# Fixing the order of TensorE's work in a 64-expert stage with issue dependencies

## The chip, the cores and the metric

The kernel runs on one core of a Trainium2 chip. The time is the device time of the whole program in microseconds, the median of three runs. Beside it stands one profiled execution, from which all rows below come; times in it count from the first instruction.

## The reference, cut to what matters

The program is a block with a mixer and a mixture of experts, followed by two attention layers. The change touches the experts alone. There are 512 tokens of width 1024 and 64 experts; each token goes to two experts, and each expert computes

```
hdn = silu(xblk @ w1[e]) * (xblk @ w3[e])      # 1024 -> 512, twice
y   = hdn @ w2[e]                              # 512 -> 1024
moe = zeros.at[buf_tok].add(yb * buf_w)        # back to the tokens, weighted
```

Every expert's three matrices are float32, 2 MiB each, so the stage reads 384 MiB of weights, whatever the routing.

## The kernel before, in words

`experts()` takes the 64 experts as 32 pairs. A pair holds 64 slots of each of its two experts, 128 rows in all. What a pair does on TensorE (PE):

- **Gather** (`gather`, L994): the pair's token rows are picked by a product of the tokens, split in a high and a low part (`n2h`, `n2l`), with a one-hot matrix `ohr` that `select` (L975 to L982) builds on VectorE. It is done for two pairs at once: 8 column blocks x 2 parts x 4 token blocks = 64 products with 256 columns, into the PSUM tag `pgat` of two buffers, copied out to `xT` by ScalarE (L996).
- **Half-width products** (`pair`): `up` (L1050) multiplies the gathered rows with `w1` and `w3` into `ph`, `down` (L1081) the gated hidden rows with `w2` into `py`. Each product has 64 stationary columns, one half of the array for each expert. A step of `up` or `down` uses one loaded tile `wraw` of 1 MiB and makes four products, which the trace counts as eight matrix instructions. A pair has 8 steps of `up` and 4 of `down`.
- **Turn** (`turn`, L1069): four transposes of the gated hidden rows, between `up` and `down`.
- **Spread** (`spread`, L1003): four transposes of the one-hot matrix per pair give `S`, used to bring results back.
- **Combination** (`combine`, L1108, L1109): for two pairs at once, 8 tiles `pcomb` of four full-width products with 512 columns, each added to `acc` by VectorE (L1111). The tag `pcomb` has two buffers. Its operands `yh` and `yl` are made from `py` by `weigh`: VectorE (L1095), ScalarE (L1096), VectorE (L1097).

The tiles `wraw` are loaded from the queue of SP by `eload` (L1029), one transfer of 1 MiB at a time, into a ring of `RAW = 10` buffers; a transfer waits until the step that used its buffer ten loads earlier is done.

The text of the program gives one order, with a small clock of its own: `later(d, f)` runs `f` after `d` more steps. In it, the work of two pairs is: six `up` steps of an odd pair, the combination of the two pairs that ended before and the gather for the next two, two `up` steps, the spread, four `down` steps of the pair before, eight `up` steps of the next pair, four `down` steps. The order that runs is not that of the text: the tile scheduler places each engine's instructions by its own model of time and by data dependencies. `tc.issue_after(ins)` adds a dependency of order alone, with no semaphore: what is traced inside the block stands behind `ins` on the same engine.

Of the kernel before, what the change touches and what calls it, by code (L numbers as in the profile page):

```python
# [10 lines left out]
F32 = mybir.dt.float32  # L11
# [7 lines left out]
P = 128  # L19
T = 512  # L20
NT = T // P
D = 1024
KD = D // P
# [23 lines left out]
class Kernel:  # L47
    def __init__(self, tc, I, out):
        self.tc, self.nc, self.I, self.out = tc, tc.nc, I, out
        self.rawn = 2048  # L50


    def f(self, name="f", dt=F32, shape=None):
# [914 lines left out]
    def select(self, first, n, sg):  # L968
# [10 lines left out]
        def task(j):  # L979
            u = self.op.tile([P, n * P], F32, tag="oh", name="oh", bufs=4)  # L980
            nc.vector.tensor_scalar(u, io, sg[:, 1, j:j + 1], None, op0=ALU.is_equal)  # L981
            nc.vector.scalar_tensor_tensor(r[:, j].rearrange("t n s -> t (n s)"), io, sg[:, 0, j:j + 1], u, op0=ALU.is_equal, op1=ALU.add)  # L982
        return r, [lambda j=j: task(j) for j in range(NT)]

    def gather(self, oh, n, xT):

        nc = self.nc
        per = 4 // n
        for k0 in range(0, KD, per):
            ps = self.pg.tile([P, per, n, P], F32, tag="pgat", name="pgat")  # L990
            for k in range(per):
                for half, src in enumerate((self.n2h, self.n2l)):
                    for j in range(NT):
                        nc.tensor.matmul(ps[:, k], src[j][:, k0 + k], oh[:, j].rearrange("t n s -> t (n s)"),  # L994
                                         start=half + j == 0, stop=half == 1 and j == NT - 1)
            nc.scalar.copy(xT[:, k0:k0 + per], ps)  # L996

    def spread(self, oh, i, later, loop):

        nc = self.nc  # L1000
        pS = self.pc.tile([P, T], F32, tag="pcomb", name="pcomb")
        for j in range(NT):
            nc.tensor.transpose(pS[:, j * P:(j + 1) * P], oh.bitcast(F32)[:, j, i], self.ident)  # L1003
        S = self.op.tile([P, T], R32, tag="S", name="S", bufs=4 if loop is None else 1)
        later(1, lambda: nc.scalar.activation(S, pS, AF.Copy))
        return S
# [25 lines left out]
    def pair(self, x, ws, later, done, loaded=()):  # L1032


        nc = self.nc
        mm = nc.tensor.matmul
        st, loaded = {}, list(loaded)
        own = [slice(64 * e, 64 * e + 64) for e in range(2)]

        def raws(w, c):  # L1040
            return loaded.pop(0) if loaded else self.eload(ws[w], w, c)

        def up(w, c):
            raw = raws(w, c)
            if c == 0:
                st[w] = self.ph.tile([P, 512], F32, tag=f"ph{w}", name="ph")
            for i in range(2):
                k = 2 * c + i
                for e in range(2):
                    mm(st[w][own[e]], x(k)[:, own[e]], raw[:, e, i], start=k == 0, stop=k == KD - 1, skip_group_check=True)  # L1050
            if c == 3:
                if w == 0:
                    later(1, act)
                else:
                    later(1, gate)
                    later(2, turn)
                    later(3, turned)

        def act():
            st["t"] = self.ep.tile([P, 512], F32, tag="silu", name="silu")  # L1060
            nc.scalar.activation(st["t"], st[0], AF.Silu)

        def gate():
            nc.vector.tensor_tensor(st["t"], st["t"], st[1], op=ALU.mult)  # L1064

        def turn():
            st["pt"] = self.pg.tile([P, 4, P], F32, tag="pgat", name="pht")
            for k in range(4):
                nc.tensor.transpose(st["pt"][:, k], st["t"][:, k * P:(k + 1) * P], self.ident)  # L1069

        def turned():
            st["hT"] = self.ep.tile([P, 4, P], F32, tag="hT", name="hT")
            nc.scalar.copy(st["hT"], st["pt"])

        def down(c):
            raw = raws(2, c)
            if c == 0:
                st["y"] = [self.py.tile([P, 512], F32, tag="py", name="py") for _ in range(2)]
            for q in range(2):
                for e in range(2):  # L1080
                    mm(st["y"][q][own[e]], st["hT"][:, c, own[e]], raw[:, e, 0, q * 512:(q + 1) * 512],  # L1081
                       start=c == 0, stop=c == 3, skip_group_check=True)
            if c == 3:
                later(1, lambda: done(st["y"]))
        return [lambda w=w, c=c: up(w, c) for w in range(2) for c in range(4)], [lambda c=c: down(c) for c in range(4)]

    def weigh(self, py, wcol, later):
# [12 lines left out]
    def combine(self, pairs):  # L1100

        nc = self.nc
        for j in range(NT):
            for q in range(2):
                ps = self.pc.tile([P, T], F32, tag="pcomb", name="pcomb")
                o = slice(q * 512, (q + 1) * 512)
                for i, (S, yh, yl) in enumerate(pairs):
                    nc.tensor.matmul(ps, S[:, j * P:(j + 1) * P], yh[:, o], start=i == 0, stop=False)  # L1108
                    nc.tensor.matmul(ps, S[:, j * P:(j + 1) * P], yl[:, o], start=False, stop=i == len(pairs) - 1)  # L1109
                a = self.acc[:, j, o]  # L1110
                nc.vector.tensor_tensor(a, a, ps, op=ALU.add)  # L1111

# [8 lines left out]
    def experts(self):  # L1121
        nc, I = self.nc, self.I
# [23 lines left out]
        sel, S = {}, {}  # L1146
# [33 lines left out]
        with self.tc.For_i(0, trips, 1):  # L1180
# [12 lines left out]
            for q in range(2):  # L1193
                b, e, ei = lt([P, 1], f"lb{q}"), lt([P, 1], f"le{q}"), lt([P, 1], f"lei{q}", I32)
# [6 lines left out]
            t = lt([P, NT, 64], "lt")  # L1201
# [16 lines left out]
            for k in range(2):  # L1218
                for j in range(NT):
# [3 lines left out]
                                     stop=k == 1 and j == NT - 1)  # L1223
# [9 lines left out]
            flush()  # L1233
            V.tensor_scalar(cur, cur, 1.0, None, op0=ALU.add)
        yield
        self.nload = nload

        prev = []
        for pr in range(32):
# [790 lines left out]
```

## Time and profile before

| | |
|---|---|
| median of three runs | 3038.85 us (3027.07 to 3040.16) |
| profiled execution | 3034.57 us, its span 3032.9 us |
| span before the expert stage | 0 to 862 us |
| expert stage | 862 to 1905 us |
| attention layers | 1905 to 3032.9 us |

The stage's borders are read from the loads of weights (the first that the stage itself issues, at 862 us) and the last product of a combination (1901 us). Share of busy time counts an engine's instructions; a pause of PE between two of its instructions shows only where no instruction runs. In the rows, PE is the matrix products, PEld the loads of their stationary operand, SPq the queue of SP's transfers, and PEclk the granted TensorE clock as a share of the full one.

### The profile page before, as it was taken

To read this page: it belongs to the slowest core of one execution; us is meant where nothing else is said; L and a number is where in the kernel's file an instruction comes from. 1 tells how busy PE (TensorE), PEld (TensorE's weight loads), DVE (VectorE), ACT (ScalarE), POOL (GpSimd) and SP (SyncE) were. 2 spreads that over 40 slices of the span, in tenths; PEclk is the share of its full clock that TensorE was granted. 3 is DMA by queue.
4 is the path that set the end of the run, shared out by engine and by line. 5 is a ranking of instruction groups with operands and counts; after the bars stand their busy time and mean duration, and the time that the engine had idled before them with its cause. 6 is when DMAs were issued, how large, how long until landed. Compare 5 with 4: busy or idle time off the path is not lost.

```text
span 3032.9 us, 37454 instructions
## 1 busy us (share of the span) xinstructions
PE 2847.4 (94%) x14006; PEld 1954.3 (64%) x14006; DVE 1579.9 (52%) x2830; ACT 1099.6 (36%) x2216; POOL 588.1 (19%) x698
## 2 busy tenths in 40 slices
PE   6989999899879999999999999799999999999999
PEld 5877878778644444444444443677888777788877
DVE  5799999646432222222222222666666456657653
ACT  4556555445311111111111111455555335546541
POOL 2257665511210000000000000623100114310001
PEclk9999999999989999999999999898999999989999
DMA  7435444374469999999999998341222344212224
GB/s 231 115 114 165 139 125 129 98 238 137 154 244 400 391 390 394 387 386 385 393 389 397 388 384 313 111 126 29 67 87 78 116 152 128 56 42 84 84 87 149
DMA packets 356786, 627.93 MB, mean 207 GB/s; under 512 B 24000, under 2 KB 205032, under 8 KB 356600
## 3 DMA queue, kind: packets, MB, share of 16 engines
q1 hardware_dynamic: 339680, 601.27, 56.4%
q10 hardware_dynamic: 14360, 15.83, 1.6%
q0 software_dynamic: 2560, 8.39, 0.8%
q8 instruction: 112, 1.84, 0.3%
q14 instruction: 74, 0.61, 0.1%
HBM read 593.95 MB, written 31.47 MB: 206 GB/s over the span
## 4 chain that ended last, share of the span: by engine, by line
PE 64%; DVE 3%; ACT 2%; DMA 1%; issue 1%; POOL 0%; SPq 0%; DVEq 0%; ACTq 0%
PE ph L1050 14%; PE py L1081 8%; PE mm L93 6%; PE mm L94 6%; PE mm L95 6%; PE pgat L994 4%; PE pcomb L1108 2%; PE pcomb L1109 2%; PE o L1549 2%; PE at L95 2%; PE at L93 2%; PE at L94 2%; PE at L1586 1%; PE at L1719 1%; PE at L1568 1%; DVE yl L1097 1%
## 5 line engine op out<-in xcount | busy, mean ns | idle before, releaser
L1050 PE MATMUL ph<-wraw,xT 128*64 128x512 f32 x2048 | 473.0, 601 | 5.6 <-DVE oh L981 5.6
L69 DVE TENSOR_TENSOR wlo<-wraw,whi 128x512 fp32r<-128x512 f32 x466 | 367.4, 796 | 202.4 <-ACT whi L68 189.0
L68 ACT ACTIVATE whi<-wraw 128x512 fp32r<-128x512 f32 x466 | 287.1, 627 | 342.3 <-PE mm L94 262.0
L1050 PEld LDWEIGHTS ph<-wraw,xT 128*64 128x64 f32 x2048 | 137.1, 137 | 270.9 <-issue 267.2
L1081 PE MATMUL py<-wraw,hT 128*64 128x512 f32 x1024 | 240.4, 601 | 0.0
L93 PE MATMUL mm<-hh,whi 128*128 128x512 f32 (+1 forms) x560 | 229.9, 411 | 1.1 <-ACT ga L1649 1.1
L94 PE MATMUL mm<-hl,whi 128*128 128x512 f32 (+1 forms) x560 | 227.4, 406 | 0.0
L95 PE MATMUL mm<-hh,wlo 128*128 128x512 f32 (+1 forms) x560 | 226.3, 404 | 0.0
L93 PE MATMUL mm<-n1h,whi 128*128 128x512 f32 x448 | 183.7, 410 | 24.3 <-DVE c L387 12.1
L1095 DVE SCALAR_TENSOR_TENSOR ys<-py,wslot,g 128x512 f32<-128x512 f32 x64 | 48.0, 751 | 286.0 <-PE py L1081 282.5
L1111 DVE TENSOR_TENSOR acc<-acc,pcomb 128x512 f32<-128x512 f32 x128 | 86.6, 687 | 208.2 <-PE pcomb L1109 208.2
L1292 POOL MEMSET invt<- 128x1 f32 x32 | 1.0, 99 | 942.0 <-DMA wraw<-in_w_dram 942.0
L95 PE MATMUL mm<-n1h,wlo 128*128 128x512 f32 x448 | 180.5, 403 | 0.0
L94 PE MATMUL mm<-n1l,whi 128*128 128x512 f32 x448 | 180.2, 403 | 0.0
L547 DVE SCALAR_TENSOR_TENSOR ucvp<-upad,dwh,ucvp 128x512 f32<-128x512 f32 x232 | 173.4, 747 | 3.7 <-ACT ucvp L541 2.2
L1064 DVE TENSOR_TENSOR silu<-silu,ph 128x512 f32<-128x512 f32 x32 | 22.0, 688 | 258.9 <-PE ph L1050 258.9
L1081 PEld LDWEIGHTS py<-wraw,hT 128*64 128x64 f32 x1024 | 65.7, 136 | 109.6 <-issue 101.4
L93 PEld LDWEIGHTS mm<-hh,whi 128*128 128x128 f32 (+1 forms) x560 | 106.5, 190 | 25.9 <-ACT ga L1649 2.5
L95 PEld LDWEIGHTS mm<-hh,wlo 128*128 128x128 f32 (+1 forms) x560 | 106.3, 190 | 25.5
L94 PEld LDWEIGHTS mm<-hl,whi 128*128 128x128 f32 (+1 forms) x560 | 106.5, 190 | 22.7
L93 PEld LDWEIGHTS mm<-n1h,whi 128*128 128x128 f32 x448 | 87.4, 195 | 45.3 <-DVE c L387 13.6
L93 PE MATMUL mm<-yh,whi 128*128 128x512 f32 x256 | 101.0, 409 | 16.1 <-ACT gb L1649 7.0
(648 smaller groups left out, 6294.2 us busy)
## 6 DMA issues: line engine op xcount, KB each, us to landing
wraw<-in_w_dram SPq DMA_DIRECT2D x384, 1024.0 KB
wraw<-in_w_in_dram SPq DMA_DIRECT2D x164, 512.0 KB
wada<-in_w_ada_dram SPq DMA_DIRECT2D x96, 256.0 KB
wraw<-in_w_ssm_out_dram SPq DMA_DIRECT2D x32, 256.0 KB
wraw<-in_cmp_w_dram SPq DMA_DIRECT2D x16, 512.0 KB
wraw<-in_w_out_dram SPq DMA_DIRECT2D x16, 512.0 KB
zd<-z ACTq DMA_DIRECT2D x32, 128.0 KB
z<-zd SPq DMA_DIRECT2D x16, 256.0 KB
```

What stands on the lines that cost most here:

```text
L68: self.nc.scalar.activation(hi, v, AF.Copy)
L69: self.nc.vector.tensor_sub(lo, v, hi.bitcast(F32))
L93: mm(ps, lh, rh, start=start, stop=False)
L94: mm(ps, lh, rl, start=False, stop=False)
L95: mm(ps, ll, rh, start=False, stop=stop)
L547: nc.vector.scalar_tensor_tensor(st[-1], u[:, k:k + T], self.dwh[:, 8 * k + m:8 * k + m + 1], st[0], op0=ALU.mult, op1=ALU.add)
L994: nc.tensor.matmul(ps[:, k], src[j][:, k0 + k], oh[:, j].rearrange("t n s -> t (n s)"), start=half + j == 0, stop=half == 1 and j == NT - 1)
L1050: mm(st[w][own[e]], x(k)[:, own[e]], raw[:, e, i], start=k == 0, stop=k == KD - 1, skip_group_check=True)
L1081: mm(st["y"][q][own[e]], st["hT"][:, c, own[e]], raw[:, e, 0, q * 512:(q + 1) * 512], start=c == 0, stop=c == 3, skip_group_check=True)
L1108: nc.tensor.matmul(ps, S[:, j * P:(j + 1) * P], yh[:, o], start=i == 0, stop=False)
L1109: nc.tensor.matmul(ps, S[:, j * P:(j + 1) * P], yl[:, o], start=False, stop=i == len(pairs) - 1)
L1111: nc.vector.tensor_tensor(a, a, ps, op=ALU.add)
```

## The change

All full-width work of the expert stage (gather, spread, combination) is put behind the last half-width product traced so far, and every half-width product behind the last full-width one traced so far. So the two kinds follow each other on PE as they do in the text. The products themselves, their number, shapes and operands stay. The transposes of `turn` get no such dependency. `self.half` and `self.whole` are emptied ahead of the loop over the pairs.

```
+    def behind_all(self, last):
+        return self.tc.issue_after(last.ins) if last and self.nload is not None else nullcontext()
...
     def gather(self, oh, n, xT):
...
-                        nc.tensor.matmul(ps[:, k], src[j][:, k0 + k], oh[:, j]...)
+                        with self.behind_all(self.half):
+                            self.whole = nc.tensor.matmul(ps[:, k], src[j][:, k0 + k], oh[:, j]...)
...
     def spread(self, oh, i, later, loop):
...
-            nc.tensor.transpose(pS[:, j * P:(j + 1) * P], oh.bitcast(F32)[:, j, i], self.ident)
+            with self.behind_all(self.half):
+                self.whole = nc.tensor.transpose(pS[:, j * P:(j + 1) * P], oh.bitcast(F32)[:, j, i], self.ident)
...
     up and down in pair():
-                    mm(st[w][own[e]], x(k)[:, own[e]], raw[:, e, i], ...)
+                with self.behind_all(self.whole):
+                    self.half = mm(st[w][own[e]], x(k)[:, own[e]], raw[:, e, i], ...)
...
     def combine(self, pairs):
...
+                with self.behind_all(self.half):
+                    for i, (S, yh, yl) in enumerate(pairs):
+                        nc.tensor.matmul(ps, S[:, j * P:(j + 1) * P], yh[:, o], ...)
+                        self.whole = nc.tensor.matmul(ps, S[:, j * P:(j + 1) * P], yl[:, o], ...)
...
     in experts(), ahead of the loop over the pairs:
-        self.nload = nload
+        self.nload, self.whole, self.half = nload, None, None
```

## Rows read from the trace of the kernel before

**Rows 1.** The page's span in 40 equal slices; busy tenths, then GB/s.

```profile
PE   6989999899879999999999999799999999999999
DMA  7435444374469999999999998341222344212224
GB/s 231 115 114 165 139 125 129 98 238 137 154 244 400 391 390 394 387 386 385 393 389 397 388 384 313 111 126 29 67 87 78 116 152 128 56 42 84 84 87 149
```

**Rows 2.** Waits of PE's weight loads, 865 to 1902 us: total, times, longest.

```profile
PEld pht L1069 <- DVE silu L1064: 27.9, 16, 1.7
PEld ph L1050 <- DMA wraw<-in_w_dram: 1.1, 3, 0.4
```

**Rows 3.** Waits of SP's transfer queue, 865 to 1880 us: total, times, longest.

```profile
SPq L1029 <- PE ph L1050: 520.7, 252, 6.2
```

**Rows 4.** Busy time of each engine in stretches of the expert stage.

```profile
core 0: us, PE busy (x) PEld busy (x) DVE busy (x) ACT busy (x) POOL busy (x), PEclk, DMA share, GB/s
874.00:1875.00 1001.00, 974.75 (x4704) 423.11 (x4702) 230.35 (x398) 119.80 (x185) 0.98 (x32) 1.00 1.01 392
874.00:962.00 88.00, 87.14 (x452) 41.09 (x450) 15.50 (x31) 12.12 (x20) 0.00 (x0) 1.00 1.03 409
1193.90:1258.60 64.70, 63.03 (x306) 27.42 (x306) 15.18 (x25) 7.81 (x12) 0.00 (x0) 1.00 1.01 388
1287.00:1306.00 19.00, 18.93 (x87) 6.92 (x85) 7.18 (x15) 2.56 (x4) 0.00 (x0) 1.00 0.97 345
1888.00:1898.00 10.00, 7.13 (x17) 4.87 (x18) 6.12 (x21) 2.39 (x5) 2.07 (x5) 0.66 0.00 1
```

**Rows 5.** PE in order of time, 1272 to 1326 us: start, length, work.

```profile
1277.61 1.94 PE L1050 MATMUL ph<-wraw,xT 128*64 128x512 f32 x8
...
1280.61 1.94 PE L1050 MATMUL ph<-wraw,xT 128*64 128x512 f32 x8
...
1282.81 0.39 PE L1109 MATMUL pcomb<-yl,S 128*128 128x512 f32 x1
...
1284.20 0.39 PE L1109 MATMUL pcomb<-yl,S 128*128 128x512 f32 x1
...
1298.85 5.37 PE L1081 MATMUL py<-wraw,hT 128*64 128x512 f32 x24
...
1306.22 0.73 PE L1108 MATMUL pcomb<-yh,S 128*128 128x512 f32 x2 [0.28 <-ACT yh L1096]
1307.48 0.73 PE L1109 MATMUL pcomb<-yl,S 128*128 128x512 f32 x2 [0.53 <-DVE yl L1097]
...
1321.24 0.66 PE L1069 MATMUL pht<-ident,silu 128*128 128x128 f32 x4 [0.86 <-DVE silu L1064]
...
1322.21 0.63 PE L994 MATMUL pgat<-ohr,n2l 128*128 128x256 f32 x4
1322.68 0.63 PE L994 MATMUL pgat<-ohr,n2h 128*128 128x256 f32 x4
```

**Rows 6.** Waits of PE's weight loads in one period, 1193.88 to 1258.6 us.

```profile
PEld pcomb L1108 <- issue: 4.1, 5, 0.8
PEld pgat L994 <- issue: 3.2, 4, 0.8
...
PEld pht L1069 <- DVE io L975: 0.8, 1, 0.8
```

**Rows 7.** VectorE in order of time, 1240 to 1310 us.

```profile
1284.63 0.69 DVE L1111 TENSOR_TENSOR acc<-acc,pcomb 128x512 f32<-128x512 f32 x1 [0.23 <-PE pcomb L1109]
```

**Rows 8.** PE in order of time at the stage's end.

```profile
1882.18 5.37 PE L1081 MATMUL py<-wraw,hT 128*64 128x512 f32 x24
1889.55 0.73 PE L1108 MATMUL pcomb<-yh,S 128*128 128x512 f32 x2 [2.00 <-ACT yh L1096]
...
1894.26 0.63 PE L1109 MATMUL pcomb<-yl,S 128*128 128x512 f32 x1
1894.69 0.63 PE L1108 MATMUL pcomb<-yh,S 128*128 128x512 f32 x1
```

More of the change, by code (lines that the diff above doesn't have):

```diff
@@ L50, in __init__ @@
         self.rawn = 2048
+        self.half = self.whole = None
     def f(self, name="f", dt=F32, shape=None):
@@ L993, in gather @@
                     for j in range(NT):
-                        nc.tensor.matmul(ps[:, k], src[j][:, k0 + k], oh[:, j].rearrange("t n s -> t (n s)"),
-                                         start=half + j == 0, stop=half == 1 and j == NT - 1)
+                        with self.behind_all(self.half):
+                            self.whole = nc.tensor.matmul(ps[:, k], src[j][:, k0 + k], oh[:, j].rearrange("t n s -> t (n s)"),
+                                                          start=half + j == 0, stop=half == 1 and j == NT - 1)
             nc.scalar.copy(xT[:, k0:k0 + per], ps)
@@ L1046, in up @@
                 st[w] = self.ph.tile([P, 512], F32, tag=f"ph{w}", name="ph")
-            for i in range(2):
+            for i, e in [(i, e) for i in range(2) for e in range(2)]:
                 k = 2 * c + i
-                for e in range(2):
-                    mm(st[w][own[e]], x(k)[:, own[e]], raw[:, e, i], start=k == 0, stop=k == KD - 1, skip_group_check=True)
+                with self.behind_all(self.whole):
+                    self.half = mm(st[w][own[e]], x(k)[:, own[e]], raw[:, e, i], start=k == 0, stop=k == KD - 1, skip_group_check=True)
             if c == 3:
@@ L1078, in down @@
                 st["y"] = [self.py.tile([P, 512], F32, tag="py", name="py") for _ in range(2)]
-            for q in range(2):
-                for e in range(2):
-                    mm(st["y"][q][own[e]], st["hT"][:, c, own[e]], raw[:, e, 0, q * 512:(q + 1) * 512],
+            for q, e in [(q, e) for q in range(2) for e in range(2)]:
+                with self.behind_all(self.whole):
+                    self.half = mm(st["y"][q][own[e]], st["hT"][:, c, own[e]], raw[:, e, 0, q * 512:(q + 1) * 512],
                        start=c == 0, stop=c == 3, skip_group_check=True)
@@ L1106, in combine @@
                 o = slice(q * 512, (q + 1) * 512)
-                for i, (S, yh, yl) in enumerate(pairs):
-                    nc.tensor.matmul(ps, S[:, j * P:(j + 1) * P], yh[:, o], start=i == 0, stop=False)
-                    nc.tensor.matmul(ps, S[:, j * P:(j + 1) * P], yl[:, o], start=False, stop=i == len(pairs) - 1)
+                with self.behind_all(self.half):
+                    for i, (S, yh, yl) in enumerate(pairs):
+                        nc.tensor.matmul(ps, S[:, j * P:(j + 1) * P], yh[:, o], start=i == 0, stop=False)
+                        self.whole = nc.tensor.matmul(ps, S[:, j * P:(j + 1) * P], yl[:, o], start=False,
+                                                      stop=i == len(pairs) - 1)
                 a = self.acc[:, j, o]
```

## The prediction

> **What bounds the kernel now.** I read the page's slices first. Slices 13 to 24 (from about 910 us to 1820 us) show PE and DMA both at nine tenths or more and a steady 385 to 400 GB/s [rows 1]. Two engines are full there, so shares of busy time can't say which of them sets the pace; the waits must.
>
> The waits of PE's weight loads name the loads of weights three times in a thousand microseconds, 1.1 us in all [rows 2]. The transfer queue, the other way round, waits 520.7 us for `up` alone to release its buffers [rows 3]. So PE is the pace and the transfers follow it. But how far behind are they? The table by stretches answers: from 874 to 962 us, when buffers were still free, the transfers ran at 409 GB/s; over the whole of 874 to 1875 us they made 392; in 1287 to 1306 us, where PE combines, 345 [rows 4]. At 409 GB/s a tile of 1 MiB takes 2.56 us. Two pairs need 24 of them: 61.5 us. One such period on PE lasts 64.7 us (the stretch 1193.9 to 1258.6 is one: its mean of 388 GB/s makes 24 tiles) [rows 4]. So a faster PE is worth 3.2 us per period, 5%, and no more. That ceiling is the most important number here.
>
> **Where PE's 64.7 us go.** Work first, from starts in order of time. A half-width matrix instruction takes (5.37 - 1.94) / 16 = 0.2144 us, a combination product (1284.20 - 1282.81) / 6 = 0.232, a gather product (1322.68 - 1322.21) / 4 = 0.118 [rows 5]. Per period: 192 x 0.2144 = 41.2; 32 x 0.232 = 7.4; 64 x 0.118 = 7.6; 16 transposes, priced like gather products, 1.9. Sum 58.1 us. So 6.6 us are neither.
>
> A change of kind is what costs them. Between two half-width steps that have four combination products between them lie 1280.61 - 1277.61 = 3.00 us [rows 5]; their work is 8 x 0.2144 + 4 x 0.232 = 2.64. A trip to full width and back thus costs 0.36 us. In one period the weight loads pause 0.8 us or more on entering full width 14 times (seven rows, of which the two longest and the last stand in [rows 6]): 14 x 0.36 = 5.0 us. What is left, 1.6 us, are waits for operands that are asked for too early: 0.86 us for `silu` ahead of a turn, 0.53 us for `yl` in a combination that follows its own pair's products directly, and 0.28 for its `yh` [rows 5]; the small rest I leave unnamed.
>
> **What the change does, part by part.** Every product stays, so the 58.1 us stay.
>
> *Fewer changes of kind.* In the text's order a period has one batch (combination and gather fall on the same step), one spread, and a turn for each pair: four trips, 1.4 us in place of 5.0.
>
> *Combination later.* It now stands six `up` steps behind the end of its pairs, 6 x 1.72 = 10 us. The waits for `yh` and `yl` (0.8 us) go. Nothing is late in their place: `acc` is read only at the stage's end.
>
> *Gather later.* In the text it stands six steps before its pair's first `up`: 10 us for ScalarE's copies, which follow PE's groups already. The one-hot tile is built on ticks ahead of it, so I cost this at nothing. If that cover were gone, every half-width product behind the gather would wait too, since they are now ordered behind it.
>
> *The turn* has no new dependency; its wait for `silu` of 0.86 us occurred 16 times before, once per period [rows 2, 5]. Bounds: 0 if it slips behind one `down` step, 1.7 if both pairs pay. I take 0.9, as now.
>
> *Eight combination tiles in a row* on two PSUM buffers are not shown before beyond two in a row. VectorE's add starts 0.04 us after the tile's last product and takes 0.69 [rows 5, 7]. A buffer's loop is 4 x 0.232 + 0.16 (tail of the last product) + 0.04 + 0.69 = 1.82 us, against 1.86 us of PE work for two tiles. That is almost level: I take 0.05 us per tile, 0.4 in all; below it is nothing, above it is a full add for each of six tiles, 4.1.
>
> PE's new period: 58.1 + 1.4 + 0.9 + 0.4 = **60.8 us**, between 59.5 (no waits) and 65.3 (58.1 + 1.4 + 1.7 + 4.1, every wait at its upper end).
>
> *The transfers.* No load is moved in SP's order, none is added. A batch (15.0 us and 0.36) releases no buffer; in 15.4 us six tiles land. The ring has ten, so the queue starves only if more than four were landed when the batch begins. If PE is the faster side it has used what has landed by then. So the period is the larger of 60.8 and 61.5: **61.5 us**, set by the transfers, and PE waits a little for data ahead of each batch.
>
> The Trainium skill, in DMA: Bandwidth & Descriptors, section "Where 436 GB/s comes from", says that about 358 GB/s from HBM bind a core for such loads, which would speak against any gain: 25.2 MB would take 70 us per period. The trace differs: its 409 GB/s stand in [rows 4], and the measurement decides.
>
> **The sum.** From 874 to 1875 us the same bytes at 409 in place of 392 GB/s take 1001 x (1 - 392/409) = 41.6 us less. To this comes the stage's end. Now the last `down` ends at 1882.18 + 5.37 = 1887.5 [rows 8], 12 us behind the last load, because PE had ten buffers of backlog. When the transfers are the bound, the last step follows its load: at least 2 us behind. The last batch holds a combination alone, 7.8 us, and the ten steps behind it catch up 10 x (2.56 - 1.72) = 8.4. I take 6 us behind: a gain of 6 (0 to 10). The final combination and the attention layers stay. Total 48 us, from the profiled execution's 3034.6: **2987 us**. The median of the runs shown is 4 us above that execution, and they span 13 us; 0.5%, 15 us, is about what a measurement here can tell from no change.
>
> **Rivals.**
>
> *PE stays the bound* (chance 0.18). The batch's waits are larger than I took: PE's period lies between 61.5 and 64.7. At 62.5 the gain is 15 periods x 2.2 = 33 us, 3002 us; at 64.2 it is 7 us. For it: the level loop of the two `pcomb` buffers, never seen with eight tiles. Against it: the add has 0.23 us of idle time ahead of it where two tiles stand in a row [rows 7], so there is a little room.
>
> *No gain* (0.10), 3035 us: the transfers already bind, and PE's saved time turns into waits for data. For it: DMA's share is 1.01 in the whole stretch. Against it: in 1287 to 1306 us that share is still 0.97 at 345 GB/s [rows 4], so the share says only that something was in flight. Here too belongs that the order hardly changes; against that, gathers now run between steps of `down`, which the new dependencies forbid.
>
> *Slower* (0.07): the waits for data cost PE its clock. At the stage's end PE waited 2.00 us, and afterwards combination products stood 0.43 us apart (1894.69 - 1894.26) [rows 8], with a mean granted clock of 0.66 in that stretch [rows 4]: the lower level. When the transfers lead, PE idles up to 2.56 - 1.72 = 0.84 us at each of the last steps ahead of a batch. At the lower clock a step takes 3.43 us, more than a load; PE falls behind until the clock is back. It decides from 7.8 us at the lower clock per period (they cost 3.9 us, all that the change saves); at 10 us a period is 65.8 and the time 15 x 1.1 = 17 us more, 3052 us. Against it: the pauses of 0.86 us for `silu` occur in stretches whose granted clock is 1.00 [rows 4, 5]. The Trainium skill, in TensorE: Matmul & The Clock Gate, section "A second HAM failure mode: psum-queue depth-cycling", says that short idle spells between groups of products can make the clock swing; by that the time would be above the present one, and the pauses at clock 1.00 do not agree.
>
> **How the numbers follow.** My forecast has 0.65: transfers set the pace, 2976 to 2997 us (0 to 10 us for the end, some 2 us for the rounding of the rates, and the runs' own spread). With PE as the bound the times go from 2997 to the present. The range of 2974 to 3012 takes in the forecast and the larger half of that case, and leaves out no change and slower. Faster by over 0.5%: 0.65 and 0.15 of PE's 0.18, 0.80; within 0.5%: 0.12; slower: 0.08.
>
> **What would show it.** Right: between two batches PE shows 24 half-width steps broken only by spread and turns; four entries into full width per period; the transfers hold 405 to 410 GB/s all through the stage, with no dip; PE's weight loads now wait for `wraw`, 0.5 to 2 us per period; the period is 61.5 us; the last load lands near 1833 us and the last `down` ends a few microseconds later. Wrong: combination tiles 1.1 us or more apart in the batch; dips below 360 GB/s during batches (the ring is full); a granted clock below 1.00 between 900 and 1830 us; or wide work still scattered over the period. If all of this is right and the time is still not near 2987, the scheduler has moved something in the layers behind the stage.

## The result, and the profile after

The changed kernel takes 2989.47 us (median of four runs, 2985.28 to 3000.34) against 3035.74 us in the runs of before beside them: a ratio of 0.9857, 95% interval 0.9821 to 0.9892. Timed a second time, with five runs, it took 2989.53 us, ratio 0.9837 (0.9817 to 0.9858). The profiled execution took 2985.28 us with a span of 2983.6, 49.3 us less than the one of before.

The page's slices of the changed kernel, to be laid beside [rows 1]: busy tenths of PE and DMA, then GB/s.

```profile
PE   6989999899969999999999998899999999999999
DMA  7435444365459999999999997341232343212224
GB/s 235 117 113 163 136 133 125 103 222 156 141 202 409 409 408 406 406 405 405 406 407 406 404 405 286 116 121 32 68 89 85 121 146 120 57 50 78 85 89 152
```

The expert stage now runs at 404 to 409 GB/s throughout. Up to 862 us the two profiles agree (PE is busy for 761.9 us of it before and 761.3 now). From there to the last combination product the stage took 1039 us before (to 1901.0) and takes 994 us now (to 1856.1): 45 of the 49 us. The other 4 lie in the attention layers behind it, which the change doesn't touch. In four profiles, of the changed kernel taken twice and of two orders of the experiments (chain_all, chain_turn), those layers took 1127.5, 1129.4, 1131.2 and 1133.7 us, and 1131.9 before, so I count these 4 as spread.

The stretches that answer to [rows 4], with the same columns: the stage, and one period of two pairs.

```profile
874.00:1833.00 959.00, 946.24 (x4696) 445.56 (x4694) 231.59 (x398) 120.39 (x185) 0.98 (x32) 1.00 1.02 407
1195.62:1257.77 62.15, 61.30 (x307) 29.10 (x305) 15.26 (x25) 7.91 (x12) 0.00 (x0) 1.00 1.02 406
```

A period is 62.15 us; before it was 64.7. But which engine sets it? The waits of PE's weight loads, 865 to 1856 us (those of before: [rows 2]):

```profile
PEld pht L1076 <- DVE silu L1071: 26.0, 15, 1.7
...
PEld ph L1057 <- DMA wraw<-in_w_dram: 1.5, 3, 0.8
...
PEld py L1088 <- DMA wraw<-in_w_dram: 0.3, 1, 0.3
```

PE waits for loaded weights 1.8 us in the whole stage, not 0.5 to 2 us per period as I had forecast. PE is still the bound, just above the transfers. Why it needs 62.15 us and not the 60.8 of my sum shows in its order of time over one period (start, length, work; most rows of the batch left out):

```profile
1185.22 10.47 PE L1057 MATMUL ph<-wraw,xT 128*64 128x512 f32 x48
1195.62 0.50 PE L1116 MATMUL pcomb<-yh,S 128*128 128x512 f32 x1
...
1209.56 0.40 PE L1000 MATMUL pgat<-ohr,n2l 128*128 128x256 f32 x2
1209.88 1.93 PE L1057 MATMUL ph<-wraw,xT 128*64 128x512 f32 x6
1211.74 0.50 PE L1116 MATMUL pcomb<-yh,S 128*128 128x512 f32 x1
...
1212.87 2.79 PE L1057 MATMUL ph<-wraw,xT 128*64 128x512 f32 x10
1215.59 1.09 PE L1010 MATMUL pcomb<-ident,ohr 128*128 128x128 f32 x8
1216.61 6.22 PE L1088 MATMUL py<-wraw,hT 128*64 128x512 f32 x26
1222.76 0.66 PE L1076 MATMUL pht<-ident,silu 128*128 128x128 f32 x4
1223.35 1.50 PE L1088 MATMUL py<-wraw,hT 128*64 128x512 f32 x5
...
1239.87 0.65 PE L1076 MATMUL pht<-ident,silu 128*128 128x128 f32 x4 [0.85 <-DVE silu L1071]
1240.45 7.09 PE L1088 MATMUL py<-wraw,hT 128*64 128x512 f32 x32
```

The reader is to see two things. First, the batch is not quite whole: seven of the eight combination tiles stand in it, mixed with the gather, and the eighth stands alone behind six half-width instructions, at 1211.74. A half-width product is put behind the last full-width product *traced*, and that is a gather product; each product of the batch in turn is put behind the last half-width one ahead of it. Nothing orders the combination tiles against the gather or the half-width products behind. That is a fifth trip to full width and back.

Second, six instructions (three products) take 1.93 us, as long as eight do in [rows 5]. Ten take 2.79 us where 1.94 and two more at 0.2144 us give 2.37 us. The weight loads show what is missing, here at the ends of four runs of half-width products:

```profile
1209.88 0.20 PEld L1057 LDWEIGHTS ph<-wraw,xT 128*64 128x64 f32 x4
1210.37 0.14 PEld L1057 LDWEIGHTS ph<-wraw,xT 128*64 128x64 f32 x1 [0.29 <-issue]
1210.80 0.14 PEld L1057 LDWEIGHTS ph<-wraw,xT 128*64 128x64 f32 x1 [0.29 <-issue]
...
1213.78 0.14 PEld L1057 LDWEIGHTS ph<-wraw,xT 128*64 128x64 f32 x2 [0.28 <-issue]
1214.21 0.14 PEld L1057 LDWEIGHTS ph<-wraw,xT 128*64 128x64 f32 x1 [0.29 <-issue]
1214.63 0.14 PEld L1057 LDWEIGHTS ph<-wraw,xT 128*64 128x64 f32 x1 [0.29 <-issue]
...
1221.38 0.14 PEld L1088 LDWEIGHTS py<-wraw,hT 128*64 128x64 f32 x1 [0.28 <-issue]
1221.81 0.14 PEld L1088 LDWEIGHTS py<-wraw,hT 128*64 128x64 f32 x1 [0.29 <-issue]
...
1237.14 0.14 PEld L1057 LDWEIGHTS ph<-wraw,xT 128*64 128x64 f32 x2 [0.28 <-issue]
1237.57 0.14 PEld L1057 LDWEIGHTS ph<-wraw,xT 128*64 128x64 f32 x1 [0.29 <-issue]
1237.99 0.14 PEld L1057 LDWEIGHTS ph<-wraw,xT 128*64 128x64 f32 x1 [0.29 <-issue]
```

Inside a run the loads come in twos every 0.43 us, one for each half of the array. At the end of a run with an odd number of products the last two come singly, still 0.43 us apart: the product that lost its partner takes the time of both. Each product is two such instructions, each in a slot of 0.43 us that could have held two, so a lone product costs 2 x 0.2144 = 0.43 us more. The stray tile leaves one on either side of it. The turn at 1222.76 cuts a step after 13 of 16 products and leaves one ahead of it; it also puts the pairs behind it out of step, so the run of 70 instructions (35 products) up to the turn at 1239.87 ends with another. Four lone products are 1.72 us per period.

The trips to full width and back are not all of one price. Take a stretch from one run of half-width products to the next, and subtract the half-width work, the full-width work and the lone product; the trip is left. It is 0.35 us for the stray tile (1209.88 to 1212.87: 2.990 - 1.286 - 0.928 - 0.429), 0.26 for the turn (1216.61 to 1223.35: 6.740 - 5.574 - 0.472 - 0.429) and 0.22 for the spread (1212.87 to 1216.61: 3.740 - 2.144 - 0.944 - 0.429). I take 0.35 for the batch and the stray tile and 0.25 for the spread and the two turns. The wait for `silu` puts PE back by 0.93 us (1223.35 to 1240.45: 17.10 less 15.01 for the 70 instructions, 0.47 for four transposes, 0.43 for the lone product and 0.26 for the trip).

With these the sum closes: 58.1 + 2 x 0.35 + 3 x 0.25 + 4 x 0.43 + 0.93 = 62.2, measured 62.15.

The stage's end, where [rows 8] stand before:

```profile
1832.71 10.78 PE L1088 MATMUL py<-wraw,hT 128*64 128x512 f32 x48
...
1845.49 0.73 PE L1116 MATMUL pcomb<-yh,S 128*128 128x512 f32 x2 [0.85 <-ACT yh L1103]
```

The last `down` ends at 1843.5, 44 us earlier than before. The rate of 400 GB/s ends in both profiles with the expert loads, at 1875 us before and at about 1837 us now, so the last `down` ends some 7 us behind the last load where it was 12.

### The profile page after: what moved, and what is told of

The parts are those of the page before. It is cut to its first block, busy times and chain, and to the rows that moved or that the text cites. A ratio compares the mean times of both kernels' runs of the same rounds, so it can differ in the third digit from the quotient of the medians.

```text
span 2983.6 us, 37486 instructions
## 1 busy us (share of the span) xinstructions
PE 2814.2 (94%) x14006; PEld 1973.6 (66%) x14006; DVE 1578.4 (53%) x2830; ACT 1101.1 (37%) x2216; POOL 589.5 (20%) x698
## 4 chain that ended last, share of the span: by engine, by line
PE 65%; DVE 2%; DMA 1%; ACT 1%; issue 1%; POOL 0%; SPq 0%; DVEq 0%; ACTq 0%
PE ph L1057 15%; PE py L1088 8%; PE mm L94 6%; PE mm L95 6%; PE mm L96 6%; PE pgat L1000 4%; PE pcomb L1116 2%; PE o L1558 2%; PE pcomb L1117 2%; PE at L96 2%; PE at L94 2%; PE at L95 2%; PE at L1595 1%; PE at L1728 1%; PE at L1577 1%; PE pht L1076 1%
## 5 line engine op out<-in xcount | busy, mean ns | idle before, releaser
L1057 PEld LDWEIGHTS ph<-wraw,xT 128*64 128x64 f32 x2048 | 151.9, 137 | 297.5 <-issue 294.0
L1088 PEld LDWEIGHTS py<-wraw,hT 128*64 128x64 f32 x1024 | 73.5, 137 | 136.4 <-issue 135.0
L1002 ACT COPY xT<-pgat 128x512 f32<-128x512 f32 x64 | 37.5, 587 | 239.6 <-PE pgat L1000 239.6
```

Of the source, the lines that this page charges most:

```text
L1057: self.half = mm(st[w][own[e]], x(k)[:, own[e]], raw[:, e, i], start=k == 0, stop=k == KD - 1, skip_group_check=True)
L1088: self.half = mm(st["y"][q][own[e]], st["hT"][:, c, own[e]], raw[:, e, 0, q * 512:(q + 1) * 512], start=c == 0, stop=c == 3, skip_group_ch ...
```

## The experiments

Eleven further runs follow: ten other kernels, and the changed one again. In five of them the transfers were taken away, to read PE's own period: the expert weights are loaded into the first ten buffers alone and read from there ever after, so these kernels leave out all later weights.

```
     def eload(self, srcs, kind, c, raw=None):
+        if raw is None and self.nload is not None and self.nload >= RAW:
+            old, of = self.kept[self.nload % RAW]
+            self.nload += 1
+            if (of == 2) == (kind == 2):
+                return old
...
```

The period is the distance of the spread's first transpose from that of the next period, averaged over the last twelve.

**pe_after**: the changed kernel without those loads.

> The changed kernel with the expert weights loaded only into the first ten buffers and read from there ever after, so the transfers are gone and the result is not the reference's. PE's order in a period is that of the changed kernel. Theory A (the prediction's: transfers set the changed kernel's period): without them the period falls from 62.15 us to PE's own 60.8 us. Theory B (PE is still the bound): it stays at 62.1 us, because PE loses 1.3 us per period to half-width products that run alone where a batch or a turn cuts a step after an odd number of them.

Measured: 61.24 us, with no transfer in flight:

```profile
1195.62:1256.86 61.24, 61.24 (x305) 29.09 (x304) 15.25 (x25) 7.91 (x12) 0.00 (x0) 1.00 0.00 1
```

Neither number was met. The scheduler placed one turn differently here, and PE has no wait for `silu` in this kernel's waits. The changed kernel without its delay of 0.93 us would be at 61.22; so the transfers cost it nothing that shows, and theory A falls. The runs of half-width products are odd in four places here too, as theory B needs, though its own 1.3 us stood for three.

**pe_chain** and **chain_all**: the same strict order without and with the loads. Every product of gather, spread, combination, `up` and `down` is put behind the one traced before it:

```
-                            self.whole = nc.tensor.matmul(ps[:, k], src[j]...)
+                            self.half = self.whole = nc.tensor.matmul(ps[:, k], src[j]...)
...
-                    self.half = mm(st[w][own[e]], ...)
+                    self.half = self.whole = mm(st[w][own[e]], ...)
...
     spread and down alike; in combine each of the two products of a pair by itself
```

> As the run before it (weights loaded once, result not the reference's), and every product of gather, spread, combination, up and down is put behind the one traced before it, so a batch is whole and cuts between steps only. Theory A: 60.8 us per period or a little less (one stray trip of 0.36 us gone). Theory B: 62.15 - 1.3 - 0.36 = 60.5 us.

Measured: 60.34 us, near theory B's 60.5, but not by B's sum. Two lone products stay, at the two turns; no turn waits for `silu`; and the whole batch waits 0.35 us for its adds: 62.15 - 0.35 - 2 x 0.43 - 0.93 + 0.35 = 60.36. So this run alone does not decide between the theories.

> The changed kernel with every product of gather, spread, combination, up and down behind the one traced before it. Theory A (transfers already set the changed kernel's period): 61.5 to 62.1 us per period and the same time, about 2985 to 2990 us. Theory B (PE is the bound at 62.15 us, 1.3 us of it from lone half-width products and 0.36 us from a stray trip): PE would need 60.5 us, so now the transfers bind at 61.5 us, PE's loads of stationary operands wait for data about 1 us per period, and the time falls by 15 x 0.65 = 10 us against the changed kernel, to about 2978 us.

Measured: 61.88 us per period, 2986.21 us (five runs), ratio 0.9831 (0.981 to 0.9853). PE alone needs 1.5 us less than that, so here the transfers do bind; the waits of PE's weight loads name `wraw` for 29.5 us now (900 to 1820 us; 1.5 in the changed kernel). The period fell by 0.27 us and not by 0.65: 24 tiles in 61.88 us are 407 GB/s and not my 409. In time that is 4 us at most, which two medians 3 us apart can't settle.

**pe_trips**: strict order without loads, three tiles apart.

```
-                later(6, lambda: self.combine(group))
+                for t in range(3):
+                    later(3 + t, lambda t=t: self.combine(group, [t]))
+                later(6, lambda: self.combine(group, range(3, 8)))
```

> As the strict order without loads (result not the reference's), but three of the eight combination tiles stand alone behind the third, fourth and fifth up step: three more trips to full width and back. By the prediction's price of a trip, 3 x 0.36 = 1.1 us more per period than the strict order. The rival that the pauses at a change only fill other slack gives 0.

Measured: 61.30 us, 0.96 more than the strict order for three trips: 0.32 us each, against the 0.36 of the prediction. The batch that is left has five tiles in a row and waits 0.11 us less for its adds, so a trip alone is 0.35.

**pe_odd**: strict order without loads, the eighth tile behind three of four products of the next `up` step.

```
                     self.half = self.whole = mm(st[w][own[e]], ...)
+                if 2 * i + e == 2 and self.hold:
+                    self.hold.pop()()          # the eighth tile of the combination
```

> As the strict order without loads (result not the reference's), but the eighth combination tile stands behind three of the four products of the next up step, an odd cut. One trip more is 0.36 us. Theory B adds two lone half-width products at 0.43 us each: 1.2 us more per period than the strict order in all. If lone products cost nothing: 0.36 us more.

Measured: 61.58 us, 1.24 more. One trip explains 0.35 of it; the odd cut is the rest, two lone products at 0.43.

**only_gather** and **only_combine**: one part of the change alone.

```
     only_gather, in combine:
-                with self.behind_all(self.half):
+                with nullcontext():
...
     only_combine, in gather and spread:
-                        with self.behind_all(self.half):
+                        with nullcontext():
```

In both, the products that lost the dependency no longer set `self.whole`, so half-width products do not stand behind them either.

> The changed kernel without the dependencies of the combination: gather and spread are ordered, combination floats in seven pieces. Nine trips per period by its static order: 58.1 + 9 x 0.36 + 0.9 = 62.2 us per period if trips are what costs, about 62 to 63 us; if the gain came from the gathers alone, 62.15 us as the changed kernel; if from the combination alone, 64.7 us as before.

> The changed kernel without the dependencies of gather and spread: combination in one batch, gather in five pieces between steps of down. Eight trips per period: 58.1 + 8 x 0.36 + 0.9 + 0.4 = 62.3 us per period if trips are what costs. If the gain came from the gathers' batch alone, 64.7 us as before.

Measured: 62.96 us (3006 us in one run) and 61.85 us (2991 us in one run). In the period the gathers alone bring two thirds of the gain, the combination alone all of it, and more than both together: its order has eight trips, but no stray tile and no odd cut, since its pieces stand between whole steps. One run each can't show that difference in the time. In only_gather the combination still follows its own pairs too early, as before:

```profile
1252.40 0.73 PE L1116 MATMUL pcomb<-yh,S 128*128 128x512 f32 x2 [0.29 <-ACT yh L1103]
```

**ring6**: the strict order with six buffers of weights.

```
-RAW = 10
-LOADED = 7
+RAW = 6
+LOADED = 5
```

> The strict order with a ring of six buffers of weights in place of ten. By the prediction's account a batch of 15.4 us takes up six tiles, so six buffers run out just at its end and the queue then starves until the first step has released one: about 2 us more per period, 63.5 us, with a dip of the transfer rate behind each batch. If the ring's depth does not matter with this order: 61.5 us as with ten.

Measured: 70.3 us per period, 3112 us in one run, 75 us above the median of before beside it. Stretches around one batch (the batch stands between the end of the `up` step of 1240.00, about 1241.9 us, and 1257.39 us):

```profile
1242.00:1251.00 9.00, 9.00 (x43) 6.78 (x44) 5.51 (x8) 0.00 (x0) 0.00 (x0) 1.00 1.02 406
1251.00:1254.00 3.00, 3.00 (x27) 3.00 (x27) 0.00 (x0) 0.86 (x2) 0.00 (x0) 1.00 0.88 351
1254.00:1257.00 3.00, 3.00 (x28) 3.00 (x27) 0.00 (x0) 0.90 (x2) 0.00 (x0) 1.00 0.07 26
1257.00:1260.00 3.00, 3.00 (x16) 1.17 (x17) 0.00 (x0) 0.58 (x1) 0.00 (x0) 1.00 0.00 0
1260.00:1263.00 3.00, 3.00 (x20) 1.43 (x18) 1.58 (x4) 1.09 (x2) 0.00 (x0) 1.00 0.84 242
1263.00:1269.00 6.00, 6.00 (x30) 2.09 (x28) 2.03 (x7) 0.10 (x1) 0.00 (x0) 1.00 0.93 353
1269.00:1275.00 6.00, 6.00 (x30) 2.01 (x28) 2.73 (x3) 1.54 (x2) 0.00 (x0) 1.00 1.02 414
```

The queue runs dry at 1254, not at the batch's end: 406 GB/s for 12 us are 4.7 tiles, since one of the six had nearly landed when the batch began. It stays dry until a step behind the batch has ended (1257.39 + 1.7) and the next transfer, issued at 1259.37, has got under way, after 1260. Then the rate swings: from 1261 to 1269 us it is 258, 406, 356, 315, 389, 377, 270 and 410 GB/s in steps of 1 us. The loads are issued one by one in this time, as steps release buffers (1261.09, 1263.97, 1265.69, 1267.41 us), so few are in flight. My expectation, 2 us, left out both ends.

**chain_turn, after_again, pe_turn**: the strict order with the turn's transposes in the chain, in the loop over the pairs alone, with and without loads; beside it the changed kernel again.

```
             for k in range(4):
-                nc.tensor.transpose(st["pt"][:, k], ...)
+                with self.behind_all(self.half):
+                    self.half = self.whole = nc.tensor.transpose(st["pt"][:, k], ...)
```

> The strict order in the loop over the pairs alone (the first gather stays free), with the transposes of the turn in the same chain, so no step is cut after an odd number of products. PE alone would need 58.1 + 4 x 0.36 + some 0.3 = 59.8 us per period. If the transfers bind below 62 us, as the strict order showed at 61.9 on average, the period stays at 61.7 to 61.9 us and the time is 2981 to 2986 us; if PE's own time still counted, the period would be near 60 us and the time about 2957 us.

> The changed kernel, timed beside the run before it on the same chip: 62.15 us per period and 2985 to 2992 us; the gap to the run before it is 15 x 0.3 = 5 us if the transfers bind there, over 25 us if PE does.

> The order of the run before last with the expert weights loaded only into the first ten buffers (result not the reference's). If a lone half-width product costs 0.43 us, and one turn per period cut a step after 13 of 16 products in the strict order, the period is 60.37 - 0.43 = 59.9 us; if the cut cost nothing, 60.4 us.

Measured: 61.81 us and 2987.93 us (2982.06 to 2989.38), ratio 0.9829 (0.981 to 0.9849); 62.15 us and 2989.53 us; 59.49 us without loads. PE's own need fell by 0.85 us against the strict order, two lone products and not the one expected, for the first odd cut leaves the second turn's pairs out of step too. With the loads nothing of it is left in the time. What PE saves it now waits; its weight loads and PE's order of time in chain_turn, with its stretch of the stage:

```profile
PEld ph L1057 <- DMA wraw<-in_w_dram: 41.4, 38, 2.3
```

```profile
1254.69 1.94 PE L1057 MATMUL ph<-wraw,xT 128*64 128x512 f32 x8 [0.71 <-DMA wraw<-in_w_dram]
1257.16 1.94 PE L1057 MATMUL ph<-wraw,xT 128*64 128x512 f32 x8 [0.53 <-DMA wraw<-in_w_dram]
```

```profile
962.00:1800.00 838.00, 816.66 (x4136) 378.51 (x4136) 205.09 (x352) 108.59 (x165) 0.98 (x32) 1.00 1.03 408
```

All periods in one table. The account adds to 58.1 us of work: the trips, first those to a combination or a gather at 0.35 us, then those to a turn or a spread at 0.25; the lone products at 0.43 us; the wait of combination tiles in a row for their two buffers (adds); and the delays, by which a late operand puts PE's next product back. A delay is 0.93 us for `silu` and 1.16 for `yh` and `yl`, more than the idle time in brackets, because the length shown for a product (0.39 us) is more than the 0.232 us behind which the next one can start.

```
kernel          trips  lone  adds  delays  account   measured, us per period
before         11 + 3     0  0       2.09    64.79     64.74
changed         2 + 3     4  0       0.93    62.20     62.15
only_gather     6 + 3     0  0       2.09    63.04     62.96
only_combine    5 + 3     0  0.35    0.93    61.88     61.85
without loads:
pe_after        2 + 3     4  0       0       61.27     61.24
pe_odd          2 + 3     4  0.35    0       61.62     61.58
pe_trips        4 + 3     2  0.24    0       61.35     61.30
pe_chain        1 + 3     2  0.35    0       60.41     60.34
pe_turn         1 + 3     0  0.35    0       59.55     59.49
with loads, PE below the transfers (account: PE alone):
chain_all       1 + 3     2  0.35    -       60.41     61.88
chain_turn      1 + 3     0  0.35    -       59.55     61.81
```

The prices are read from these same traces, so the table shows that they fit together; what tests them are the steps between kernels that differ in one thing, pe_trips, pe_odd and pe_turn against pe_chain.

Three orders on which PE alone differs by 1.75 us (pe_after, pe_chain, pe_turn) end within 0.34 us of each other when the loads are there.

## Why the prediction was right, and where it was not

*PE was the pace and the transfers a ceiling 5% above it*: right. Orders that free PE further stop at 61.8 to 61.9 us; my 61.5 took a rate of 409 GB/s where 24 tiles per period came at 407.

*A trip costs 0.36 us and 14 of them make up most of what is not work*: right for trips to a combination or a gather (0.35), shown by three trips added alone, and by the account over nine kernels. Trips to a turn or a spread cost 0.25, so the 14 are 4.6 us and not 5.0; the waits that I put at 1.6 us are 2.1.

*Four trips are left*: five, because nothing tied the combination to the half-width products behind it. Small, 0.35 us.

*PE's new period of 60.8 us*: this term was mis-sized, since it held no price for an odd cut. Four lone products (1.72 us) and the stray trip (0.35) were missing, while the adds on two buffers (0.4) did not occur in this order and three of the trips were 0.11 us too dear: 60.8 + 1.72 + 0.35 - 0.4 - 0.33 = 62.1, measured 62.15. So the step "the period is 61.5 us, set by the transfers, and PE waits for data" failed as a statement on the changed kernel: PE is the bound there, which was the first rival, by its smallest margin. Of the signs named ahead, the rate without a dip came (404 to 409 GB/s); the four entries and the waits for `wraw` in every period did not. The time hardly tells the two apart, since 62.15 and 61.8 us are 0.35 us apart: 15 periods of 64.7 - 62.15 are 38 us, where the transfers' ceiling gave 41.6. That the time was met to 3 us is to this extent luck: PE's period happened to end just above the ceiling.

*The stage's end, 6 us*: right in size; the last `down` follows its load 5 to 6 us closer. 38 and 5 to 6 are 43 to 44 of the 45 us measured in the stage.

*The adds on two `pcomb` buffers*: in chain_all, where eight tiles do stand in a row, two take 1.98 us (1198.61 to 1200.59 in its order of time) against 1.86 of work: 0.06 us a tile, as taken (0.05). In the changed kernel the scheduler mixed tiles and gather, and the wait is gone.

*The ring of ten is deep enough*: right, with less room than I had reckoned. The queue must last the batch, one step more and the start of a transfer; six buffers cost 8.4 us per period against ten.

*The lower clock* did not come: in chain_turn PE pauses mostly 0.5 to 0.7 us (once 1.45) ahead of some of the last steps before a batch, 24 us in all from 900 to 1820 us, and the granted clock of the stage is 1.00. *No gain* is excluded by the interval.

Open is how much of the 1.6 to 3.3 us by which the strict orders were faster in the median is real: the runs of one kernel span 5 to 15 us. In the profiles the last combination ends at 1853.8 us (chain_turn) and 1855.9 (chain_all), with the changed kernel at 1856.1 and 1858.6; the layers behind it differ by up to 6 us from profile to profile, which hides such a gain. Why a trip costs what it does, and why one to a turn or a spread costs less, no run here shows.

## What to carry to other kernels

When two resources are both at nine tenths, look for the waits to find the pace and for the undisturbed rate of the other to find the ceiling: here it fixed the gain to within 10 us, although the sum for the engine itself was off by 1.3 us per period. When products that share the array run in pairs, cut their runs only where the pairs are complete, and check what an order-only dependency doesn't order. Before gathering an engine's work into long batches, count the buffers that have to carry the transfers over the batch, its first step and the restart.

## What the runs showed of the hardware that I had not expected

A half-width product without its partner on the other half of the array takes the pair's time: instructions came singly at the same 0.43 us spacing as in twos, and one odd cut shifts the pairs of the run behind it (0.85 us for both in pe_turn).

A queue of 1 MiB loads that ran dry took some 9 us to hold its full rate again: 242 GB/s in the mean of the first 3 us, 353 in the next 6, and 414 behind that. It touched 406 GB/s in the third microsecond already, and the loads came one by one as buffers were released, so the runs don't separate a slow restart from too few loads in flight.
